# The last step of a seven-product attention block: product A12·B21 moved to the end and finished token tile by token tile, residual buffers moved, GpSimd additions dropped

## The chip, the cores and the metric

One core of one Trainium2 chip runs the whole program. The metric is device time in microseconds (us) of one execution. The kernel before takes 910.19 us, the median of 3 runs (908.84 to 910.43).

## The reference

One layer of neighbourhood attention over 512 tokens (8 rows of 64) with 16 heads of 128, model width 2048, all in float32:

```python
h = rms_norm(x, norm_pre[i])
q, k, v, z = jnp.split(h @ w_in, 4, axis=-1)      # w_in: 2048 x 8192
o = neighbourhood_attention(q, k, v, rpb)
y = (o * jax.nn.silu(z)) @ w_out                  # w_out: 2048 x 2048
x = x + rms_norm(y, norm_post[i])
```

What this case is about is the end: the right half of `y = g @ w_out`, the sum of squares of each row of y, and `x + y * rstd * gain`.

## The kernel before

**Products.** Every float32 operand is split into hi (rounded for TensorE) and lo (the rest), and a product is hi·hi + lo·hi + hi·lo, three matmuls of 128x512 for each tile of 128 tokens. ScalarE makes hi (L231), VectorE makes lo (L232). Ten steps run one behind the other, 512 *slots* in all. Steps 0 and 8 are plain products. Step 9, `LAST`, makes columns 1024 to 2047 of y as a 2x2 block product in seven passes of eight slots (KH = 8, six matmuls per slot); a pass multiplies one combination of blocks of A (the gated attention output) by one combination of blocks of B (w_out). The passes go in this order: A11, S1, A12, N2, A22, N4, N3. Passes 0 and 2 add into chain X in PSUM, 1, 3 and 5 into Y, 4 and 6 into Z (`chain`, L248). `combine` (L317) takes what a chain holds after each pass.

**Operands.** `T[k]` holds a running combination of weight blocks: VectorE adds a freshly loaded block `raw` to it in passes 1, 3 and 4 (L223) and in pass 5 (L239). The `raw` tiles are a ring of four (NRAW), so the load of one waits until the one four earlier has been used up; hi and lo are rings of three. `prep(m)` makes the operands of slot m and is written two slots ahead (AHEAD). The combinations of A stay in SBUF in tiles `a{k}_0` (A11, N4, S1), `a{k}_1` (A12, A22) and `a{k}_2` (N2, N3).

**The end.** Columns of y are four quarters n = 0 to 3 of 512, tokens four tiles t of 128. Step 8 leaves quarters 0 and 1. In step 9, pass A12 completes quarter 2 of tiles 0 and 1, pass N4 quarter 3 of the same tiles, and pass N3 quarters 2 and 3 of tiles 2 and 3. `finish(n, t)` (L646) squares and sums a quarter on ScalarE and multiplies it by the gain on VectorE; with the fourth quarter GpSimd makes the factor `rcy`. `final(t)` (L660) adds the residual: three quarters by one VectorE instruction (L668), the quarter q = 1 by ScalarE (L665) and a GpSimd addition (L666); then the output DMA (L670). In the last pass, the eight slots of tile 2 come first and then the eight of tile 3 (L286 to L292); its operands `w{m}` lie in `a{k}_0`.

**Queues.** All weight and residual loads and most outputs are issued by SyncE (SP), one behind the other. The residual x is loaded by `load_res` (L672), two 256 KB tiles at a time into `a{k}_1`, from slot 33 of step 9 on. A residual tile's 128 partitions read 2 KB each from rows of x that lie 64 rows (512 KB) apart; a raw or T tile is 256 KB in one piece. Engines run in the order in which their instructions stand; a scheduler orders those that the code doesn't pin.

Of the kernel before, what the change touches and what calls it, by code (L numbers as in the profile page):

```python
# [38 lines left out]

NSTEP = HEADS // 2  # L40
# [8 lines left out]
B11, B12, B21, B22 = range(4)  # L49
NRAW = 4  # L50
# [15 lines left out]
def na_block(ctx: ExitStack, tc: tile.TileContext, xT, x, gpre, gpost, w, rpb, mask, out):  # L66
# [43 lines left out]
    for k in range(KH):  # L110
        for n, ops in enumerate(((A11, N4, S1), (A12, A22), (N2, N3))):
            t = ag.tile([P, len(ops), 2, 256], F32R, tag=f"a{k}_{n}", name=f"a{k}_{n}")
            for i, o in enumerate(ops):
                AT[k, o] = (t, i)
# [25 lines left out]
    def split_a(k, src, o, scalar=None, vector=None):  # L140
# [3 lines left out]
        hi, lo = t[:, i : i + 2, 0, :], t[:, i : i + 2, 1, :]  # L144
        (scalar or nc.scalar).copy(hi, src)  # L145
        (vector or nc.vector).tensor_tensor(lo, src, hi.bitcast(F32), ALU.subtract)  # L146

    def take_x(k):
        nc.scalar.activation(X[k], X[k], AF.Copy, scale=gcol[:, k : k + 1])
        split_a(k % KH, X[k], A11 if k < KH else A12)  # L150
# [35 lines left out]
    def where(m):  # L186
# [5 lines left out]
        return step, *divmod(m, KT if step in PLAIN else KH)  # L192
# [7 lines left out]
    for i, m in enumerate(seq):  # L200
        e = max(m - 6, seq[i - NRAW] if i >= NRAW else 0)
# [14 lines left out]
    def prep(m):  # L216
# [63 lines left out]
    def mm_seven(m):  # L280
        step, p, k = where(m)
        c = chain(p)
        if p in (0, 1, 4) and k == 0:
            b = (step + (c == "Y")) % 2
            U[c] = [pm.tile([P, L], F32, tag=f"u{2 * b + s}", name=f"u{step}{c}{s}") for s in range(2)]
        if step == LAST and p == 6:  # L286
            products(m, (0,))
            if k == KH - 1:
                combine_last(0)
                for mm in range(m - KH + 1, m + 1):  # L290
                    products(mm, (1,))
                combine_last(1)  # L292
# [24 lines left out]
    def combine(step, p):  # L317
# [10 lines left out]
        elif p == 2:  # L328
            c["11"] = pair(f"c11_{step}")
            for s in range(2):  # L330
                if step == LAST:
                    finish(2, s, u[s], c["11"][:, s, :])
                else:
                    nc.scalar.activation(c["11"][:, s, :], u[s], AF.Copy, scale=rc[:, s : s + 1])
# [24 lines left out]

    def combine_last(s):  # L360
        u, c = U["Z"][s], C[LAST]
        nc.vector.tensor_tensor(c["21"][:, s, :], u, c["21"][:, s, :], ALU.subtract)
        nc.vector.tensor_tensor(c["22"][:, s, :], c["22"][:, s, :], u, ALU.subtract)
        finish(2, 2 + s, c["21"][:, s, :])
        finish(3, 2 + s, c["22"][:, s, :])
        final(2 + s)
# [386 lines left out]
```

## Time and profile before

| | |
|---|---|
| time, median of 3 runs | 910.19 us (908.84 to 910.43) |
| the profiled execution: its own time | 909.24 us |
| the profiled execution: span from first to last instruction | 907.5 us |
| PE busy share of the span | 97% |
| DVE (VectorE) busy share | 83% |
| ACT (ScalarE) busy share | 62% |
| POOL (GpSimd) busy share | 4% |

The rows are those of the profiled execution; its time is 1.7 us longer than its span and 0.95 us below the median. Times in rows are us from the start of the span. PE is TensorE's matmuls, PEld its weight loads, SPq and ACTq are the DMA issues of SyncE and ScalarE. A row with "x14" merges 14 like instructions, and its duration then runs from the first start to the last end, with the gaps.

### The profile page before, as it was taken

Reading aid. Unit: us, or ns where it says so; the run is one execution under the profiler, and the core shown is the slowest. Engines: PE = TensorE matmul, PEld = TensorE weight load, DVE = VectorE, ACT = ScalarE, POOL = GpSimd, SP = SyncE. Lnnn points to the kernel's source line nnn. Section 1 sums busy time; section 2 is a strip of 40 time slices with the busy share of each in tenths; the row PEclk is TensorE's granted clock in tenths of the full one; section 3 lists DMA queues with packets and bytes.
Section 4 is the critical chain, followed back from the end, with each engine's and each line's share of the span. In section 5 each row is a group of like instructions: output and inputs, shape, how many; then the busy total and the mean of one; then the engine's idle time right before and its main releaser. Section 6 shows DMA issues by size and latency. Waiting matters only on the chain.

```text
span 907.5 us, 13123 instructions
## 1 busy us (share of the span) xinstructions
PE 879.1 (97%) x4184; PEld 729.6 (80%) x4184; DVE 756.4 (83%) x1395; ACT 563.0 (62%) x1077; POOL 36.2 (4%) x63
## 2 busy tenths in 40 slices
PE   9999999999999999999999999999999999999981
PEld 7888888888888888888888888888878888888660
DVE  4477979897988998799879987989799756886877
ACT  6666857585658566755776576758576654455342
POOL 1000000000000000000000000000002000000003
PEclk9999999999999999999999999999999999999996
DMA  8894367637664765476546745773676334544795
GB/s 258 247 266 129 94 183 220 194 101 217 211 173 114 232 203 165 123 233 199 148 148 214 223 140 159 219 209 116 185 255 192 106 117 127 153 137 147 237 219 185
DMA packets 85877, 163.32 MB, mean 180 GB/s; under 512 B 10016, under 2 KB 10016, under 8 KB 85808
## 3 DMA queue, kind: packets, MB, share of 16 engines
q1 hardware_dynamic: 82080, 151.56, 55.8%
q0 software_dynamic: 3296, 10.41, 4.4%
q8 instruction: 32, 0.52, 0.2%
q10 hardware_dynamic: 432, 0.53, 0.2%
q14 instruction: 37, 0.30, 0.1%
HBM read 154.59 MB, written 7.86 MB: 179 GB/s over the span
## 4 chain that ended last, share of the span: by engine, by line
PE 85%; issue 5%; DMA 4%; DVE 3%; POOL 1%; ACT 1%; SPq 0%; DVEq 0%; POOLq 0%; ACTq 0%
PE u L269 19%; PE u1Y L308 4%; PE u4Y L308 4%; PE u5Y L308 4%; PE u6Y L308 4%; PE u3Y L308 4%; PE u2Y L308 4%; DMA raw<-in_w 3%; PE u1X L308 2%; PE u4X L308 2%; PE u3X L308 2%; PE u2X L308 2%; PE u7X L308 2%; PE u5X L308 2%; PE u6X L308 2%
## 5 line engine op out<-in xcount | busy, mean ns | idle before, releaser
L231 ACT CAST hi<-t 128x512 fp32r<-128x512 f32 x312 | 192.0, 618 | 134.4 <-DVE lo L232 26.0
L232 DVE TENSOR_TENSOR lo<-t,hi 128x512 fp32r<-128x512 f32 x312 | 212.8, 688 | 29.8 <-ACT hi L231 29.0
L232 DVE TENSOR_TENSOR lo<-raw,hi 128x512 fp32r<-128x512 f32 x192 | 131.7, 690 | 66.0 <-ACT hi L231 53.2
L231 ACT CAST hi<-raw 128x512 fp32r<-128x512 f32 x192 | 118.7, 620 | 103.9 <-DVE lo L232 23.5
L223 DVE TENSOR_TENSOR t<-t,raw 128x512 f32<-128x512 f32 x192 | 128.4, 688 | 6.3 <-DMA raw<-in_w 5.7
L269 PE MATMUL u<-hi,a 128*128 128x512 f32 x512 | 131.1, 392 | 1.4 <-ACT a L145 0.8
L269 PEld LDWEIGHTS u<-hi,a 128*128 128x128 f32 x512 | 95.0, 188 | 21.5 <-ACT a L145 1.3
L269 PE MATMUL u<-lo,a 128*128 128x512 f32 x256 | 70.8, 390 | 0.0
L269 PEld LDWEIGHTS u<-lo,a 128*128 128x128 f32 x256 | 48.1, 188 | 10.1
L239 DVE TENSOR_TENSOR t<-t,raw 128x512 f32<-128x512 f32 x64 | 42.9, 689 | 7.7 <-DMA raw<-in_w 7.7
L308 PE MATMUL u9Y<-hi,a 128*128 128x512 f32 x96 | 27.0, 398 | 3.6 <-ACT hi L231 3.6
L440 DVE TENSOR_TENSOR bm<-braw,mask_sb 128x256 f32<-128x256 f32 x48 | 27.5, 603 | 0.0
L308 PE MATMUL u1Y<-hi,a 128*128 128x512 f32 x96 | 26.8, 396 | 0.0
L308 PE MATMUL u4Y<-hi,a 128*128 128x512 f32 x96 | 26.8, 396 | 0.0
L308 PE MATMUL u5Y<-hi,a 128*128 128x512 f32 x96 | 26.8, 396 | 0.0
L308 PE MATMUL u3Y<-hi,a 128*128 128x512 f32 x96 | 26.8, 396 | 0.0
L308 PE MATMUL u6Y<-hi,a 128*128 128x512 f32 x96 | 26.8, 396 | 0.0
L308 PE MATMUL u2Y<-hi,a 128*128 128x512 f32 x96 | 26.8, 396 | 0.0
L308 PE MATMUL u7Y<-hi,a 128*128 128x512 f32 x96 | 26.8, 396 | 0.0
L146 DVE TENSOR_TENSOR a<-x,a 128x512 fp32r<-128x512 f32 x16 | 11.0, 690 | 18.2 <-ACT a L145 18.2
L434 POOL DMA_DIRECT2D braw<-in_rpb x16 | 8.6, 535 | 436.1 <-DVE bm L440 252.0
L308 PEld LDWEIGHTS u9Y<-hi,a 128*128 128x128 f32 x96 | 17.6, 188 | 9.2 <-ACT hi L231 5.9
(444 smaller groups left out, 1958.0 us busy)
## 6 DMA issues: line engine op xcount, KB each, us to landing
raw<-in_w SPq DMA_DIRECT2D x384, 256.0 KB, 2.9
t<-in_w SPq DMA_DIRECT2D x128, 256.0 KB, 2.9
x<-in_xT SPq DMA_DIRECT2D x16, 256.0 KB, 5.5
xres<-in_x SPq DMA_DIRECT2D x16, 256.0 KB, 8.2
graw<-zm POOLq DMA_DIRECT2D x14, 256.0 KB, 3.6
out<-xres SPq DMA_DIRECT2D x14, 256.0 KB, 3.0
sq<-in_x SPq DMA_DIRECT2D x6, 512.0 KB, 9.2
braw<-in_rpb POOLq DMA_DIRECT2D x16, 184.0 KB, 3.9
```

What stands on the lines that cost most here:

```text
L146: (vector or nc.vector).tensor_tensor(lo, src, hi.bitcast(F32), ALU.subtract)
L223: nc.vector.tensor_tensor(T[k], T[k], src, ALU.add)
L231: nc.scalar.copy(hi, src)
L232: nc.vector.tensor_tensor(lo, src, hi.bitcast(F32), ALU.subtract)
L239: nc.vector.tensor_tensor(T[k], T[k], src, ALU.add)
L269: nc.tensor.matmul(U[n][j], l, r, start=k == 0 and i == 0, stop=k == KT - 1 and i == 2)
L308: nc.tensor.matmul(U[c][s], l, r, start=p in (0, 1, 4) and k == 0 and n == 0, stop=k == KH - 1 and n == 2, skip_group_check=True,)
L434: nc.gpsimd.dma_start(raw[:, 0 : 7 * TBL + 32], src)
L440: nc.vector.tensor_tensor(bm[:, i, :].rearrange("p (a b) -> p a b", b=8), rev, mask_sb[:, i, :].unsqueeze(2).to_broadcast([P, 32, 8]), ALU ...
```

## The change

- In step 9 the passes go A11, S1, N2, A22, N4, N3, A12 (`LATE`). Quarters 2 and 3 of tiles 2 and 3 are complete after N3, one pass before the end, and quarter 2 of tiles 0 and 1 comes last.
- The last pass takes all eight slots of tile 0, finishes tile 0 (`finish`, `final`), then tile 1. Its operands hi and lo go to the storage of N2 and A22 (`m >= N - KH`), and their `prep` is written beside that of N3, one pass ahead. Chain Z moves to two other PSUM tiles, because X stays open to the end.
- `a{k}_0` is cut in two: A11 alone, and N4 with S1. The split of A's first half into hi and lo (`take`) so becomes two instructions of 256 columns per engine in place of one of 512.
- The residual is loaded one tile per call: tiles 2 and 3 from slot 8 of step 9 on into the A11 storage, tile 1 from slot 16 on into buffers `z`, tile 0 from slot 41 on.
- In `final` all four quarters are VectorE's; ScalarE's scaling and GpSimd's addition go. `finish` no longer waits for the squares before the gain multiplication of quarter 2 from PSUM.

```diff
+LATE = (0, 1, 3, 4, 5, 6, 2)
...
-        for n, ops in enumerate(((A11, N4, S1), (A12, A22), (N2, N3))):
+        for n, ops in enumerate(((A11,), (N4, S1), (A12, A22), (N2, N3))):
...
+    def take(k):
+        if k < KH:
+            split_a(k, X[k][:, 0:256], A11)
+            split_a(k, X[k][:, 256:512], N4)
+        else:
+            split_a(k - KH, X[k], A12)
...
-        e = max(m - 6, seq[i - NRAW] if i >= NRAW else 0)
+        e = max(m - 6 if m < N - KH else 0, seq[i - NRAW] if i >= NRAW else 0)
...
-        if step == LAST and p == 6:
-            t = ag.tile([P, 2, L], F32R, tag=f"a{k}_0", name=f"w{m}")
-            hi, lo = t[:, 0, :], t[:, 1, :]
+        if m >= N - KH:
+            hi, lo = (A(k, o).rearrange("p a b -> p (a b)") for o in (N2, A22))
...
+            if step == LAST and c == "Z":
+                U[c] = [px.tile([P, L], F32, tag="T", name=f"u{step}{c}{s}") for s in range(2)]
+            else:
+                U[c] = [pm.tile([P, L], F32, tag=f"u{2 * b + s}", name=f"u{step}{c}{s}") for s in range(2)]
+        if m >= N - KH:
+
+            s, kk = divmod(2 * k, KH)
+            for j in (kk, kk + 1):
+                products(N - KH + j, (s,))
+            if kk + 2 == KH:
+                finish(2, s, U["X"][s], C[LAST]["11"][:, s, :])
+                final(s)
...
+        elif step == LAST:
+            c["11"] = pair(f"c11_{step}")
+            for s in range(2):
+                dve.tensor_tensor(c["21"][:, s, :], u[s], c["21"][:, s, :], ALU.subtract)
+                dve.tensor_tensor(c["22"][:, s, :], c["22"][:, s, :], u[s], ALU.subtract)
+                finish(2, 2 + s, c["21"][:, s, :])
+                finish(3, 2 + s, c["22"][:, s, :])
...
-            if q == 1:
-                nc.scalar.activation(yg[q, t], yg[q, t], AF.Copy, scale=rcy[:, col])
-                nc.gpsimd.tensor_tensor(r, yg[q, t], r, ALU.add)
-            else:
-                nc.vector.scalar_tensor_tensor(r, yg[q, t], rcy[:, col], r, ALU.mult, ALU.add)
-            eng = nc.scalar if t == 3 and q % 2 else nc.sync
+            dve.scalar_tensor_tensor(r, yg[q, t], rcy[:, col], r, ALU.mult, ALU.add)
+            eng = nc.scalar if t == 1 and q % 2 else nc.sync
...
     for k in range(KH):
-        at(base(LAST) + 4 * KH + 1 + 3 * k // 2, load_res, k)
-    for t in range(2):
-        at(base(LAST) + 6 * KH + t, final, t)
+        t, q = divmod(k, 4)
+        at(base(LAST) + KH + k, load_res, 2 + t, q)
+        at(base(LAST) + (5 * KH + 2 * q + 1 if t == 0 else 2 * KH + 2 * q), load_res, t, q)
+    for s in range(2):
+        at(base(LAST) + 6 * KH + 1 + s, final, 2 + s)
...
     for m in range(-AHEAD, N):
-        if m + AHEAD < N:
+        if m + AHEAD < N - KH:
             prep(m + AHEAD)
+        if N - 2 * KH <= m + AHEAD < N - KH:
+            prep(m + AHEAD + KH)
```

SP's queue near the start of step 9 before; `raw470` is the weight tile of slot 470, and step 9 begins with slot 456:

```order
L212 DMA raw470_8567<-in_w 128x512
L212 DMA raw471_8582<-in_w 128x512
L212 DMA raw472_8595<-in_w 128x512
L212 DMA raw473_8608<-in_w 128x512
L212 DMA raw474_8621<-in_w 128x512
```

The same place now; `xres20` is the residual of tile 2, quarter 0:

```order
L223 DMA raw470_8607<-in_w 128x512
L64 DMA xres20_8617<-in_x 128x1x512
L223 DMA raw471_8624<-in_w 128x512
L64 DMA xres21_8632<-in_x 128x1x512
L223 DMA raw472_8639<-in_w 128x512
L64 DMA xres22_8647<-in_x 128x1x512
L223 DMA raw473_8654<-in_w 128x512
L64 DMA xres23_8662<-in_x 128x1x512
```

Twelve residual tiles have moved up: eight stand one behind each raw from raw470 to raw477, and four more between raw478 and raw485. The last four stand behind raw511, the last weight tile.

VectorE in the same stretch before (`lo466` is the lo operand of slot 466, made from T):

```order
L232 TENSOR_TENSOR lo465_8548<-t1_136,hi465_8547 128x512
L232 TENSOR_TENSOR lo466_8564<-t2_137,hi466_8563 128x512
L232 TENSOR_TENSOR lo467_8579<-t3_138,hi467_8578 128x512
L232 TENSOR_TENSOR lo468_8592<-t4_139,hi468_8591 128x512
L232 TENSOR_TENSOR lo469_8605<-t5_140,hi469_8604 128x512
```

and now:

```order
L242 TENSOR_TENSOR lo465_8588<-t1_144,hi465_8587 128x512
L234 TENSOR_TENSOR t0_143<-t0_143,raw472_8639 128x512
L242 TENSOR_TENSOR lo466_8604<-t2_145,hi466_8603 128x512
L234 TENSOR_TENSOR t1_144<-t1_144,raw473_8654 128x512
L242 TENSOR_TENSOR lo467_8621<-t3_146,hi467_8620 128x512
L234 TENSOR_TENSOR t2_145<-t2_145,raw474_8669 128x512
L242 TENSOR_TENSOR lo468_8636<-t4_147,hi468_8635 128x512
```

Between two lo operands of pass S1 there now stands the addition of a raw tile for pass N2, six slots ahead of the slot whose lo follows it.

VectorE at the end now, from the first residual additions (`u9X0` is chain X of tile 0, `u9X1` that of tile 1):

```order
L64 SCALAR_TENSOR_TENSOR xres32_8707<-s5_9_8722,rcy_154,xres32_8707 128x512
L64 SCALAR_TENSOR_TENSOR xres33_8725<-e_9_8841,rcy_154,xres33_8725 128x512
L64 TENSOR_TENSOR c11_9_9170<-u9X0_8509,gpost2_8072 128x512
L64 TENSOR_SCALAR msy_153<-part_109,ms3_152 128x1
L64 SCALAR_TENSOR_TENSOR xres00_9105<-y0_0_8118,rcy_154,xres00_9105 128x512
L64 SCALAR_TENSOR_TENSOR xres00_9105<-y1_0_8480,rcy_154,xres00_9105 128x512
L64 SCALAR_TENSOR_TENSOR xres02_9156<-c11_9_9170,rcy_154,xres02_9156 128x512
L64 SCALAR_TENSOR_TENSOR xres02_9156<-s1_9_8599,rcy_154,xres02_9156 128x512
L64 TENSOR_TENSOR c11_9_9170<-u9X1_8510,gpost2_8072 128x512
```

The finishing of tiles 2 and 3 (combinations, gains, eight residual additions) stands whole ahead of that of tile 0, and tile 0 ahead of tile 1.

## Rows read from the trace of the kernel before

**Rows 1.** The page: the span, and TensorE's busy time, share and instructions.

```profile
span 907.5 us, 13123 instructions
PE 879.1 (97%) x4184; PEld 729.6 (80%) x4184; DVE 756.4 (83%) x1395; ACT 563.0 (62%) x1077; POOL 36.2 (4%) x63
```

**Rows 2.** Busy time by stretches: the stretch, PE busy (instructions), PEld, DVE, ACT and POOL the same way, PEclk, the DMA share and GB/s.

```profile
820.00:830.00 10.00, 10.00 (x46) 8.29 (x45) 4.88 (x8) 5.76 (x10) 0.00 (x0) 1.00 0.41 114
...
850.00:860.00 10.00, 8.47 (x37) 6.11 (x35) 6.99 (x13) 3.67 (x6) 0.00 (x0) 1.00 0.89 256
860.00:870.00 10.00, 8.41 (x31) 5.53 (x32) 7.34 (x13) 3.59 (x6) 0.00 (x0) 1.00 1.06 272
870.00:880.00 10.00, 8.73 (x35) 5.89 (x33) 6.54 (x11) 3.77 (x7) 0.00 (x0) 1.00 1.06 248
```

**Rows 3.** The timeline of PE, step 9: its first matmuls and its last. Columns: start, duration, engine, line, operation, names, count.

```profile
802.62 1.07 PE L308 MATMUL u9X<-hi,a 128*128 128x512 f32 x4
...
881.94 5.86 PE L308 MATMUL u9Z<-w,a 128*128 128x512 f32 x25
```

**Rows 4.** The timeline of all engines from 885 us to the end, cut to the rows that the sum uses.

```profile
885.57 2.97 POOL L666 TENSOR_TENSOR xres<-y,xres 128x512 f32<-128x512 f32 x2
885.61 1.80 DVE L668 SCALAR_TENSOR_TENSOR xres<-c,rcy,xres 128x512 f32<-128x512 f32 x1
...
889.67 0.74 DVE L668 SCALAR_TENSOR_TENSOR xres<-c,rcy,xres 128x512 f32<-128x512 f32 x1
890.33 0.74 DVE L668 SCALAR_TENSOR_TENSOR xres<-s,rcy,xres 128x512 f32<-128x512 f32 x1
891.00 0.68 DVE L362 TENSOR_TENSOR s<-u9Z,s 128x512 f32<-128x512 f32 x1
891.60 0.67 DVE L363 TENSOR_TENSOR e<-e,u9Z 128x512 f32<-128x512 f32 x1
...
894.12 0.20 DVE L656 TENSOR_SCALAR msy<-part,ms 128x1 f32<-128x1 f32 x1
...
894.39 0.55 POOL L657 TENSOR_TENSOR rcy<-msy,mhalf 128x1 f32<-128x1 f32 x1 [5.86 <-DVE msy L656]
...
894.98 0.75 DVE L668 SCALAR_TENSOR_TENSOR xres<-y,rcy,xres 128x512 f32<-128x512 f32 x1
...
901.51 1.75 DVE L668 SCALAR_TENSOR_TENSOR xres<-e,rcy,xres 128x512 f32<-128x512 f32 x1
```

**Rows 5.** The chain of waits in order of time (start, duration, what): two of its pieces in step 9.

```profile
856.21 6.31 DMA raw<-in_w
...
871.09 8.60 DMA raw<-in_w
```

**Rows 6.** The DMA view of 856 to 872 us, its rate in 40 slices of 0.4 us.

```profile
GB/s 343 394 405 384 220 210 266 246 256 246 256 261 287 399 389 379 389 256 200 220 236 271 236 225 271 271 338 297 205 215 225 251 236 266 230 292 297 328 200 241
```

**Rows 7.** The DMA view of 871.8 to 883 us: rate in 40 slices of 0.28 us, and what was moved.

```profile
GB/s 219 219 219 271 241 256 278 234 263 219 212 278 212 205 241 271 234 285 256 249 256 219 234 241 227 212 256 241 263 263 263 249 263 183 146 132 88 37 0 0
DMA packets 1337, 2.42 MB, mean 216 GB/s; under 512 B 156, under 2 KB 156, under 8 KB 1337
```

**Rows 8.** The DMA view of 803 to 840 us: rate in 40 slices of 0.925 us, and its loads with the median time to landing.

```profile
GB/s 164 0 0 0 0 75 208 177 352 208 295 153 233 0 0 0 0 18 9 0 0 0 51 250 190 133 226 193 140 257 206 166 259 281 337 175 261 210 146 213
...
raw<-in_w SPq DMA_DIRECT2D x19, 256.0 KB, 3.0
```

**Rows 9.** The timeline of DVE and of SP's issues from 806 us: additions to T for pass S1 (L223), lo operands (L232), raw loads.

```profile
806.46 0.69 DVE L223 TENSOR_TENSOR t<-t,raw 128x512 f32<-128x512 f32 x1
...
807.18 25.01 SPq L212 DMA_DIRECT2D raw<-in_w  x14
...
811.32 0.69 DVE L232 TENSOR_TENSOR lo<-t,hi 128x512 fp32r<-128x512 f32 x1
...
811.92 0.69 DVE L223 TENSOR_TENSOR t<-t,raw 128x512 f32<-128x512 f32 x1
...
812.53 0.69 DVE L232 TENSOR_TENSOR lo<-t,hi 128x512 fp32r<-128x512 f32 x1
...
848.97 1.22 DVE L339 TENSOR_TENSOR s<-e,s 128x1024 f32<-128x1024 f32 x1
```

**Rows 10.** Groups of instructions (line, engine, operation, shapes, count, then busy us, mean ns, idle before): a subtraction of 512 columns (the page) and one of 256 (groups by shape).

```profile
L146 DVE TENSOR_TENSOR a<-x,a 128x512 fp32r<-128x512 f32 x16 | 11.0, 690 | 18.2 <-ACT a L145 18.2
```

```profile
L62 DVE TENSOR_TENSOR x<-x,x 128x256 f32<-128x256 f32 x24 | 10.2, 423 | 0.5
```

**Rows 11.** Busy time by stretches, columns as in rows 2, around the other place where A is split.

```profile
690.00:700.00 10.00, 10.00 (x51) 8.50 (x51) 9.97 (x17) 6.88 (x13) 4.36 (x8) 1.00 0.70 190
700.00:710.00 10.00, 9.48 (x42) 7.51 (x41) 9.53 (x17) 8.65 (x16) 1.09 (x2) 1.00 0.58 168
```

More of the change, by code (lines that the diff above doesn't have):

```diff
@@ L143, in split_a @@
         src = src.rearrange("p (a b) -> p a b", b=256)
-        hi, lo = t[:, i : i + 2, 0, :], t[:, i : i + 2, 1, :]
+        n = src.shape[1]
+        hi, lo = t[:, i : i + n, 0, :], t[:, i : i + n, 1, :]
         (scalar or nc.scalar).copy(hi, src)
         (vector or nc.vector).tensor_tensor(lo, src, hi.bitcast(F32), ALU.subtract)
+    def take(k):
[4 more added lines that the diff above has]
+            split_a(k - KH, X[k], A12)
     def take_x(k):
         nc.scalar.activation(X[k], X[k], AF.Copy, scale=gcol[:, k : k + 1])
-        split_a(k % KH, X[k], A11 if k < KH else A12)
+        take(k)
     def sum_x(k):
@@ L191, in where @@
             step += 1
-        return step, *divmod(m, KT if step in PLAIN else KH)
+        p, k = divmod(m, KT if step in PLAIN else KH)
+        return step, LATE[p] if step == LAST else p, k
     def is_raw(m):
@@ L284, in mm_seven @@
             b = (step + (c == "Y")) % 2
[L285 to L292, printed above, removed]
+            if step == LAST and c == "Z":
[9 more added lines that the diff above has]
+                final(s)
         else:
@@ L330, in combine @@
             for s in range(2):
-                if step == LAST:
-                    finish(2, s, u[s], c["11"][:, s, :])
-                else:
-                    nc.scalar.activation(c["11"][:, s, :], u[s], AF.Copy, scale=rc[:, s : s + 1])
+                nc.scalar.activation(c["11"][:, s, :], u[s], AF.Copy, scale=rc[:, s : s + 1])
         elif p == 3:
@@ L358, in combine @@
                 scale_c(c["22"], s, 2)
[L360 to L366, printed above, removed]
     def scale_c(t, s, j):
@@ L549, in fetch_g @@
         nc.gpsimd.dma_start(X[h], graw[h])
-    def take_g(h):
-        split_a(h % KH, X[h], A11 if h < KH else A12)
     beside = {}
@@ L608, in na_block @@
             at(early(h - 5), fetch_g, h)
-            at(early(h - 2), take_g, h)
+            at(early(h - 2), take, h)
         else:
-            at(when(h, 23), take_g, h)
+            at(when(h, 23), take, h)
     pending = {}
@@ L649, in finish @@
         y = yg[n, t] = src if dst is None else dst
-        rest = px.tile([P, L], F32, tag="S", name=f"ysq{n}_{t}") if dst is None else dst
-        nc.scalar.activation(rest, src, AF.Square, accum_out=part[:, t, n : n + 1])
-        if n == 2:
+        rest = px.tile([P, L], F32, tag="S", name=f"ysq{n}_{t}") if n > 1 else dst
+        i = n if n < 2 or t > 1 else 5 - n
+        nc.scalar.activation(rest, src, AF.Square, accum_out=part[:, t, i : i + 1])
+        (dve if n > 1 else nc.vector).tensor_tensor(y, src, gb[n], ALU.mult)
+        if i == 2:
             nc.vector.reduce_sum(ms3[:, col], part[:, t, 0:3], axis=mybir.AxisListType.X)
             nc.vector.tensor_scalar(ms3[:, col], ms3[:, col], 1.0 / D, EPS, ALU.mult, ALU.add)
-        if n == 3:
-            nc.vector.tensor_scalar(msy[:, col], part[:, t, 3:4], 1.0 / D, ms3[:, col], ALU.mult, ALU.add)
+        if i == 3:
+            dve.tensor_scalar(msy[:, col], part[:, t, 3:4], 1.0 / D, ms3[:, col], ALU.mult, ALU.add)
             nc.gpsimd.tensor_tensor(rcy[:, col], msy[:, col], mhalf[:, 0:1], ALU.pow)
-        nc.vector.tensor_tensor(y, src, gb[n], ALU.mult)
     def final(t):
```

18 lines of the change are left out of this document (11 added, 7 removed).

## The prediction

> **What bounds the kernel now.** I read the page first, then busy time by stretches, then the timeline of the last step, the chain of waits and the DMA views. TensorE is busy 97% of the span [rows 1], so only two places can give anything: where it stands still, and what comes behind its last matmul. Both are in step 9. At full pace 46 matmuls pass in the 10 us from 820 [rows 2], 0.2174 us each; a slot of six takes 1.304 us and the 56 slots of step 9 take 73.0 us. The step starts at 802.6 and PE ends at 881.94 + 5.86 = 887.8 [rows 3], so it takes 85.2: 12.2 us are lost, nearly all after 850, where the stretches hold 31 to 37 matmuls instead of 46 [rows 2]. The chain of waits names the cause: weight tiles that take 6.3 and 8.6 us to land [rows 5], against 3.0 when nothing stands ahead of them [rows 8]. The 16 residual tiles share the queue with T and raw there. Behind the last matmul lie 907.5 - 887.8 = 19.7 us, in which VectorE, ScalarE and GpSimd finish four token tiles; beside GpSimd's additions one VectorE residual addition took 1.80 us, alone 0.74 [rows 4].
>
> **The end: what the change removes and adds.** Count from E, the moment at which pass N3 is done and the last pass (48 matmuls, 10.4 us) starts. VectorE's order sets the rest. Two blocks (combine, gain, sums) for tiles 2 and 3: before, one ran from 891.00 to 894.12 with one foreign instruction of 0.6 among it [rows 4], so between 2.5 and 3.1 us; I take 2.95 since the two now stand strictly one behind the other and wait for their squares: 5.9. Eight residual additions at the pace of those that ran alone, 890.33 to 891.00, 0.67 [rows 4]: 5.3, together 11.2. Tile 0: the gain multiplication 0.6, from `msy` over GpSimd's `rcy` to the first addition 894.98 - 894.12 = 0.86 [rows 4], four additions 2.66: 4.1, at 15.3. Tile 1 the same: 19.5. PE has ended at 10.4, so tile 1's sums are there long before. From the end of the last addition to the end of the span it was 907.5 - 903.26 = 4.2 [rows 4]. So the span ends at **E + 23.7**, 13.3 us behind PE instead of 19.7. The removed GpSimd and ScalarE work costs VectorE four more additions (2.7 us); the slow ones beside GpSimd (four at some 1.0 us extra) go. Bounds: 2.5 to 3.3 per block and 0.6 to 0.7 per addition give 22.3 to 25.2.
>
> **When E comes.** Without any wait PE would reach E 48 slots after 802.6: 865.2. What can hold it up is the new place of the loads. Before, the queue was empty from 815 to 822 [rows 8]; twelve residual tiles now fill that hole and more. Their price: in 871.8 to 883, 2.42 MB = 9.2 tiles moved in about 10.5 us of traffic, mostly residual [rows 7]. Unmixed weight tiles pass at some 390 GB/s (the slices with 379 to 405 GB/s in [rows 6]), 0.68 us a tile. With two weight tiles among the 9.2, a residual tile costs (10.5 - 1.4) / 7.2 = 1.27, say 1.3 us, twice as much.
>
> The Trainium skill, page "DMA: Bandwidth & Descriptors", section "Specifications", wants 512 B per transfer for full rate, and a residual tile moves in 2 KB pieces; by that it would cost what a weight tile costs and the time would be that of the first rival below, which the rates in [rows 7] speak against. The same page, section "Latency and other measured facts", reports 207 GB/s for rows 512 KiB apart, which is how the residual is read; that would be 1.27 us a tile, so here the trace agrees.
>
> Now the queue. raw470 is issued at 807.18, since the addition at 806.46 frees its buffer [rows 9]; traffic begins near 808.4 [rows 8], so the first residual tile starts at 809.1. From it to raw485 stand 12 residual and 15 raw tiles: 12 x 1.3 + 15 x 0.68 = 25.8 us; with about 1 us from last byte to landing, raw485 lands at **835.9**. VectorE adds it to T, and in its order 37 instructions stand between the addition at 806.46 and that one; at the pace of 0.605 (811.32, 811.92, 812.53 in [rows 9]) it would be there at 828.8. So it is kept waiting about 7 us, spread over the additions of raw472 to raw485, and what is queued behind each of them is the lo operand that PE needs next. Before, PE had none of this: the S1 additions ran some ten microseconds ahead, and pass A12, which needs no addition, came next.
>
> From the addition of raw485 to the lo operand of slot 503, the last of N3, stand 51 instructions of 512 columns, one of 1024 (1.22 us [rows 9]) and four tiny ones: 30.9 + 1.2 + 0.4 = 32.5 us. This is tight, because the operands of A12 are made in the same stretch as those of N3. I add 1.5 for waits inside it: raw492 and raw506 can only be issued when the tile four earlier is used up, and at 3.0 us to landing [rows 8] each comes 0.6 to 0.9 late. Bounds 0 and 3. Then 1.0 for that lo and the four matmuls behind it. E = 835.9 + 32.5 + 1.5 + 1.0 = **870.9**, 5.7 us of stalls against 12.2 now. TensorE's granted clock stayed at 1.00, its level of 2.4 GHz, through the stalls of before [rows 2], so I price no slower clock.
>
> **Small edits.** Splitting A's first half into two halves: 2 x 0.423 in place of 0.690 [rows 10], 0.15 us for each of 16 pairs, on ScalarE about the same. The eight at the start hide while the input loads: VectorE sits idle for 18.2 us ahead of that line [rows 10]; without that cover 1.2 us. The other eight fall where VectorE is busy 9.97 and 9.53 of 10 us and PE already loses 0.5 [rows 11]: between 0 and 1.5 in all, I take **0.5**. Chain Z in other PSUM tiles, the A11 storage, and the last four residual tiles behind raw511 (needed 11 us after E) I cost at nothing: PE's last pass and VectorE's finishing of tiles 2 and 3 cover the loads; were that cover gone, the first of them would add about its 3 us of landing.
>
> **Sum.** 870.9 + 23.7 + 0.5 = 895.1 of span, plus the 1.7 outside it: 896.8 against 909.24 of the profiled execution, 12.4 less. That execution lies 0.95 below the median of 910.19; on the median's scale 897.8, say **898**. A measurement here can tell about 0.2% (1.8 us) from no change: faster means under 908.4, slower over 912.0.
>
> **Rivals.** (1) *The loads hide.* If a residual tile costs what a weight tile does, 27 x 0.68 + 809.1 + 1 = 828.5, VectorE is never kept waiting, and 828.8 + 32.5 + 1.5 + 1.0 = 863.8 lies under PE's own 865.2. Then 865.2 + 23.7 + 0.5 + 1.7 + 0.95 = 892. For it: the slices with nearly 400 GB/s [rows 6]; against: the mixed ones [rows 7]. (2) *The delay only moves.* If mixing slows every tile to the 248 GB/s of 870 to 880 [rows 2], 262 KB take 1.06 us; raw485 lands at 809.1 + 27 x 1.06 + 1 = 839, E comes 3 us later, and the eight T tiles right behind meet a queue that isn't empty yet (some 2 us): 903. Most of the old stall is then back. (3) *Slower: the ring of four starves VectorE through three passes.* A raw that takes 8.6 us [rows 5] with four in flight means one per 2.15 us where PE needs one per 1.304. If that held for the 25 raws from raw471 to raw495, 0.85 x 25 = 21.2 us, plus 1.8 because N3 then starts with VectorE full (12.2 us of work for 10.4 of matmuls): 865.2 + 23.0 + 23.7 + 0.5 + 1.7 + 0.95 = 915. It turns into a loss from 22 such raws on. Against it: only twelve residual tiles, and the four last ones stand apart. (4) *Nothing gained*: about 19 such raws, or the end isn't shortened because VectorE has taken over GpSimd's share, would leave the time within 0.2%. That the order isn't as the code says is excluded: it stands above.
>
> **How the numbers follow.** Forecast (895 to 902) 0.55, loads hide (892) 0.22, delay moves (903) 0.14, slower 0.05, no change 0.04. The range reaches to both neighbours, with the bounds of the end: 891 to 905. Faster 0.91, same 0.04, slower 0.05.
>
> **What would show it.** In the profile of the changed kernel: PE's last matmul 13 us ahead of the end, and 16 residual additions of VectorE near 0.74 us, none at 1.8; matmul counts under 46 per 10 us between about 815 and 840 with raw tiles landing late, and again near the end of N3; full counts in the last pass; VectorE without a gap from E on. Wrong would be: full counts from 815 to 840 (then rival 1), stalls reaching to 860 (rivals 2 and 3), or VectorE waiting in the last pass for residual tiles.

## The result, and the profile of the changed kernel

The changed kernel takes **902.89 us** (median of 4 runs, 901.65 to 903.68) against 909.52 (908.46 to 910.43) before: ratio 0.9926, 95% interval 0.9908 to 0.9945, 6.6 us or 0.7% faster. The prediction of 898 us had the sign right and its range, 891 to 905, holds the time, but only half of the expected gain came. A second measurement of the same kernel, beside the experiments, gave 901.76 us and the ratio 0.9926 again (0.9900 to 0.9952).

The execution profiled here took 903.68 us, 901.9 of them span. First the first matmuls of three passes, as one tile's instructions on TensorE (duration min/median/max in ns, first start to last start):

```profile
L322 PE MATMUL u1X<-hi,a x64: 389/390/486, 98.4 to 134.5; 128*128 128x512 f32 x64
L322 PE MATMUL u9X<-hi,a x32: 389/389/390, 807.2 to 817.6; 128*128 128x512 f32 x32
L322 PE MATMUL u9Y<-hi,a x96: 387/389/501, 818.1 to 865.8; 128*128 128x512 f32 x96
L322 PE MATMUL u9X<-a,a x32: 389/389/390, 878.3 to 888.7; 128*128 128x512 f32 x32
```

Three things are to be read here. Step 9 begins at 807.2, not at 802.6 as before [rows 3], and step 1 at 98.4 instead of 94.3, so some 4 us went where the change does almost nothing. The first pass of eight slots takes 818.1 - 807.2 = 10.9 us: a slot is **1.36 us**, not the 1.304 of the prediction. And the last pass starts (E) at 878.3, 71.1 us behind the start of the step, where 48 slots at full pace are 65.3: 5.8 us of stalls.

Busy time by 10 us (sum, PE with its matmuls, granted clock, DMA share, GB/s) shows the stalls, as [rows 2] does before:

```profile
810.00:820.00 10.00, 10.00 (x46) 1.00 0.69 196
820.00:830.00 10.00, 9.37 (x40) 1.00 1.06 265
830.00:840.00 10.00, 7.87 (x31) 1.00 1.00 271
840.00:850.00 10.00, 10.00 (x46) 1.00 0.75 239
870.00:880.00 10.00, 9.25 (x41) 1.00 0.51 131
```

They have moved from the stretch 850 to 882 to where the twelve residual loads now are, and come once more at the end of N3. VectorE's timeline gives the pace (start, duration, instruction, in brackets the idle time before it and who ended it):

```profile
819.05 0.69 DVE L234 TENSOR_TENSOR t<-t,raw 128x512 f32<-128x512 f32 x1 [1.26 <-DMA raw<-in_w]
821.00 0.69 DVE L234 TENSOR_TENSOR t<-t,raw 128x512 f32<-128x512 f32 x1 [0.66 <-DMA raw<-in_w]
822.99 0.69 DVE L234 TENSOR_TENSOR t<-t,raw 128x512 f32<-128x512 f32 x1 [0.69 <-DMA raw<-in_w]
824.96 0.69 DVE L234 TENSOR_TENSOR t<-t,raw 128x512 f32<-128x512 f32 x1 [0.67 <-DMA raw<-in_w]
826.95 0.69 DVE L234 TENSOR_TENSOR t<-t,raw 128x512 f32<-128x512 f32 x1 [0.69 <-DMA raw<-in_w]
...
837.10 0.69 DVE L234 TENSOR_TENSOR t<-t,raw 128x512 f32<-128x512 f32 x1 [0.96 <-DMA raw<-in_w]
```

Each addition waits for its raw tile, and they come 1.98 us apart (7.90 us over four): one raw and one residual tile, 0.68 + 1.3, the prices of the prediction. What the prediction did not foresee is at the start. Stretches of 2 us at 44 to 52 (same columns), and under them the waits there (us in total, times, longest):

```profile
44.00:46.00 2.00, 1.62 (x8) 1.00 0.99 218
46.00:48.00 2.00, 0.25 (x1) 0.95 1.02 277
48.00:50.00 2.00, 2.00 (x5) 0.50 0.41 113
50.00:52.00 2.00, 2.00 (x8) 0.70 1.01 316
```

```profile
PE u L279 <- ACT hi L241: 2.1, 1, 2.1
ACT x L159 <- DMA x<-in_xT: 1.9, 1, 1.9
```

ScalarE waits for the last x tile, the operand that TensorE needs is queued behind that, TensorE stops for 2.1 us, and then its granted clock is 0.50, the 1.2 GHz level, for some 3 us. The end of the kernel, with VectorE's last additions and the output transfers:

```profile
884.00 1.41 DVE L64 SCALAR_TENSOR_TENSOR xres<-y,rcy,xres 128x512 f32<-128x512 f32 x2
884.77 12.74 SPq L675 DMA_DIRECT2D out<-xres  x14
...
894.87 1.42 DVE L64 SCALAR_TENSOR_TENSOR xres<-y,rcy,xres 128x512 f32<-128x512 f32 x2 [0.66 <-POOL rcy L667]
896.21 0.75 DVE L64 SCALAR_TENSOR_TENSOR xres<-c,rcy,xres 128x512 f32<-128x512 f32 x1
896.87 0.75 DVE L64 SCALAR_TENSOR_TENSOR xres<-s,rcy,xres 128x512 f32<-128x512 f32 x1
```

All additions take 0.74 to 0.75 (a row with "x2" merges two), none 1.8 as in [rows 4], and the span ends 23.6 us behind E (predicted 23.7).

So the questions were: does the cut of the A tile cost the 4.6 us at the start; are the stalls the residual loads' placing; what do the order and VectorE's taking over of GpSimd's additions bring; and what bounds the tail.

### The profile page after: what moved, and what is told of

It is laid out like the page before. It is cut to its first block, busy times and chain, and to the rows that moved or that the text cites. A ratio compares the mean times of both kernels' runs of the same rounds, so it can differ in the third digit from the quotient of the medians.

```text
span 901.9 us, 13169 instructions
## 1 busy us (share of the span) xinstructions
PE 880.9 (98%) x4184; PEld 731.3 (81%) x4184; DVE 755.3 (84%) x1415; ACT 561.2 (62%) x1089; POOL 29.7 (3%) x59
## 5 line engine op out<-in xcount | busy, mean ns | idle before, releaser
L241 ACT CAST hi<-t 128x512 fp32r<-128x512 f32 x320 | 196.8, 618 | 137.3 <-DVE lo L242 31.1
L242 DVE TENSOR_TENSOR lo<-t,hi 128x512 fp32r<-128x512 f32 x320 | 218.1, 687 | 25.8 <-ACT hi L241 24.9
L242 DVE TENSOR_TENSOR lo<-raw,hi 128x512 fp32r<-128x512 f32 x184 | 125.8, 689 | 62.8 <-ACT hi L241 50.3
L241 ACT CAST hi<-raw 128x512 fp32r<-128x512 f32 x184 | 113.6, 620 | 98.9 <-PE u L279 18.7
L279 PE MATMUL u<-hi,a 128*128 128x512 f32 x512 | 133.1, 397 | 3.4 <-ACT hi L241 2.1
L149 DVE TENSOR_TENSOR a<-x,a 128x256 fp32r<-128x256 f32 (+1 forms) x24 | 11.6, 512 | 19.5 <-ACT a L148 19.5
```

Of the source, the lines that this page charges most:

```text
L241: nc.scalar.copy(hi, src)
L242: nc.vector.tensor_tensor(lo, src, hi.bitcast(F32), ALU.subtract)
L279: nc.tensor.matmul(U[n][j], l, r, start=k == 0 and i == 0, stop=k == KT - 1 and i == 2)
```

## The experiments

Every kernel was measured beside the kernel before on its chip; each ratio is to that. In this table "time" is the median of a kernel's runs; the other columns are read from its one profiled execution, which can lie some us off the median (e9's took 897.78, e4's 901.79). They are us from the span's start; "step" is E less the first matmul of u9X, 65.3 at full pace; "tail" is the end less E; "out" is the end less the first output issue.

| run | time us | u1X | u9X | E | step | tail | out |
|---|---|---|---|---|---|---|---|
| changed kernel | 902.89 | 98.4 | 807.2 | 878.3 | 71.1 | 23.6 | 17.1 |
| e7 the same again | 901.76 | 98.2 | 805.6 | 877.9 | 72.3 | 23.7 | 17.2 |
| e10 x early | 899.62 | 95.3 | 802.5 | 874.6 | 72.1 | 23.6 | 17.2 |
| e4 GpSimd back | 903.41 | 94.8 | 801.9 | 874.6 | 72.7 | 25.4 | 19.9 |
| e2 S1 apart | 901.74 | 94.7 | 804.7 | 877.9 | 73.2 | 23.6 | 17.1 |
| e11 one load in two slots | 898.70 | 95.9 | 804.8 | 875.0 | 70.2 | 23.8 | 17.3 |
| e3 one load in three slots | 894.60 | 95.7 | 803.1 | 869.4 | 66.3 | 23.6 | 17.1 |
| e8 e3, halves together | 894.89 | 95.5 | 803.1 | 869.6 | 66.5 | 23.8 | 17.3 |
| e9 e3, other finishing order | 894.63 | 98.0 | 804.9 | 872.5 | 67.6 | 23.5 | 17.0 |
| e12 e9 and x early | 893.66 | 95.2 | 803.0 | 870.9 | 67.9 | 22.8 | 16.4 |

**The cut alone** (e1), on the kernel before:

```diff
-        for n, ops in enumerate(((A11, N4, S1), (A12, A22), (N2, N3))):
+        for n, ops in enumerate(((A11,), (N4, S1), (A12, A22), (N2, N3))):
...
+    def take(k):
+        if k < KH:
+            split_a(k, X[k][:, 0:256], A11)
+            split_a(k, X[k][:, 256:512], N4)
+        else:
+            split_a(k - KH, X[k], A12)
...
-        split_a(k % KH, X[k], A11 if k < KH else A12)
+        take(k)
...
-            t = ag.tile([P, 2, L], F32R, tag=f"a{k}_0", name=f"w{m}")
+            t = ag.tile([P, 2, L], F32R, tag=f"a{k}_1", name=f"w{m}")
...
-        buf = ag.tile([P, 2, L], F32, tag=f"a{k}_1", name=f"xres{k}")
+        buf = ag.tile([P, 2, L], F32, tag=f"a{k}_2", name=f"xres{k}")
```

> The kernel before, with only the tile of the A operands cut in two, so that the first half of every A tile is split by two copies and two subtractions of 256 columns (w and the residual tiles take the names of the new tiles that they overlay); order, residual loads and final additions as before. Theory (the cut costs the start-up: ScalarE does one more copy for every x tile, the last x tile is late, and TensorE loses its clock in the gap): the first matmul of u9X moves from 802.6 us to about 807, the gap at 45 to 48 us and the granted clock of 0.5 behind it are there, and the time is 913 to 915 us. Rival (the late x tile of the changed kernel comes from the moved loads' jitter and not from the cut): first matmul of u9X at 802 to 804, no gap over 1 us at 45 to 48 us, time 908 to 911 us.

908.68 us, ratio 0.9992 (0.9972 to 1.0013). u1X starts at 95.2 and u9X at 802.8, where the kernel before has 94.3 and 802.6. The theory falls: between these two executions the cut costs 0.9 us in step 0 and 0.2 by step 9, and e5, which has no cut, starts u1X at 95.8.

**Another cut** (e2), which splits nothing at the start:

```diff
-        for n, ops in enumerate(((A11,), (N4, S1), (A12, A22), (N2, N3))):
+        for n, ops in enumerate(((A11, N4), (S1,), (A12, A22), (N2, N3))):
...
-        at(base(LAST) + KH + k, load_res, 2 + t, q)
+        at(base(LAST) + 2 * KH + k, load_res, 2 + t, q)
...
```

> The changed kernel with the A tile cut at another place: A11 and N4 stay in one tile, so that the start-up has one copy and one subtraction of 512 columns per x tile again, and S1 alone gives its room to the eight early residual loads. Since S1 is read one pass later than A11, these loads and the four of tile 1 stand eight slots later. Theory (the cut cost the start-up 4.6 us): first matmul of u9X at 802 to 804, 897 to 900 us, with 70 to 72 us from there to the last pass (stalls moved a pass later, not gone). Rival (jitter, or the cost sits elsewhere in step 0): first matmul of u9X at 806 to 808, 902 to 904 us.

901.74 us, ratio 0.9922 (0.9894 to 0.9951): no gain over the changed kernel. u1X at 94.7 is no better than with the cut (94.8 in e4); u9X at 804.7 lies between both forecasts. Between u1X and u9X this execution takes 710.0 us, the others of the table 706.9 to 708.9; e2 also splits N4 and S1, in steps 0 and 8, by two instructions each time in place of one, and whether that is the cause was not tried. The loads a pass later move the stalls by a pass and make them no smaller (7.9 us).

**The changed kernel again** (e7), unaltered.

> The changed kernel unaltered, once more beside the others. Theory (the 4.1 us lost in step 0 of the profiled execution, by the x tile that landed late at 46 us and the lower clock behind it, are one execution's and not the change's): first matmul of u1X at 94.5 to 96 and of u9X at 802 to 804 instead of 807.2, 71 to 74 us from there to the last pass, 23.6 behind it, profiled time 898.5 to 902.5; median 901 to 903. Rival (the change brings it): u1X at 98 to 99, u9X at 806 to 808.

The gap is there again, the theory's forecast missed:

```profile
L322 PE MATMUL u1X<-hi,a x64: 389/389/486, 98.2 to 134.3; 128*128 128x512 f32 x64
...
46.00:48.00 2.00, 0.53 (x2) 0.96 1.03 287
48.00:50.00 2.00, 2.00 (x6) 0.50 0.55 194
```

But its six runs fall into 903.17 to 903.51 (the profiled one among them) and 900.10 to 900.36. And e1, e3, e4, e6, e8, e9 and e11, whose instructions up to the last step are those of the changed kernel one for one, have a gap of 2 us in e9's profiled execution only (2.1); e11's has 1.2, e4's 0.8, the rest 0.4 or less. e9's profiled execution took 897.78 us, the other four of e9 893.82 to 894.87. So the gap comes in some executions of one and the same code, three of nine here, and costs some 3 us. Whether the kernel before has it as often is not known: two profiles have its start, its own without a gap and e5's with 0.3 us.

**x earlier** (e10):

```diff
-        if 0 <= m and m + 3 < KT:
-            load_x(m + 3)
+        for k in range(KT):
+            if m == (k - 3 if k < 8 else k - 4 if k < 11 else k - 5):
+                if k >= 3:
+                    load_x(k)
```

> The changed kernel with the x tiles 8 to 15 of step 0 issued one slot earlier (8 to 10) and two slots earlier (11 to 15); nothing of the last step altered. Theory (the gap at 45 to 48 us in both profiled executions of the changed kernel is the last x tile, landing 6 us after its issue among raws and squares, and the lower clock behind the gap): no gap over 0.5 us at 44 to 50 us, granted clock 1.00 there, first matmul of u1X at 94 to 95.5 instead of 98.3, 898.5 to 901 us. Rival (the raws of step 0 are what is late, and x only stands before them): the gap stays or moves, 901 to 904 us.

899.62 us, ratio 0.9904 (0.9877 to 0.9931). A gap of 1.3 us stands at 42 to 44, the clock stays at 1.00, u1X starts at 95.3:

```profile
42.00:44.00 2.00, 0.69 (x3) 1.00 0.91 229
44.00:46.00 2.00, 2.00 (x10) 1.00 0.65 191
...
L322 PE MATMUL u9X<-hi,a x32: 389/389/389, 802.5 to 812.9; 128*128 128x512 f32 x32
L322 PE MATMUL u9X<-a,a x32: 389/389/389, 874.6 to 885.0; 128*128 128x512 f32 x32
```

Time as the theory said; the gap is smaller and earlier, and not gone. Since the gap comes only in some executions, one profile without the clock's fall is no proof; the intervals of e10 and e7 overlap. For the prediction this execution is the cleanest: it starts step 9 where the kernel before does, and reaches E at 874.6.

**Residual loads spread** (e3):

```diff
-        at(base(LAST) + KH + k, load_res, 2 + t, q)
-        at(base(LAST) + (5 * KH + 2 * q + 1 if t == 0 else 2 * KH + 2 * q), load_res, t, q)
+        at(base(LAST) + KH + 3 * k, load_res, 2 + t, q)
+        at(base(LAST) + (5 * KH + 2 * q + 1 if t == 0 else 4 * KH + 3 * q), load_res, t, q)
```

> The changed kernel with the twelve early residual loads of step 9 spread: one in every three slots from slot 8 to slot 41, instead of twelve in slots 8 to 22 (the last four as they were). Theory (1.3 us of transfer per residual tile beside 0.68 per raw is more than a slot of 1.36, so the loads starve the additions of S1 and N2): from the first u9X to the last pass 66 to 68 us instead of 71.1, and 898.5 to 900.5 us. Rival (the raws come late by their own latency and ring, whatever lies beside them): 70 to 72 us there and 902 to 904 us. A third (spreading only moves the crowd to N4 and N3, where the eight raws of A12 are loaded too): the stalls show at 850 to 880, 901 to 904 us.

**894.60 us**, ratio 0.9841 (0.9813 to 0.9869), twice the gain of the changed kernel and 4 us under the theory's forecast. Its step came out as forecast; the rest is the start, where the profiled execution has a gap of 0.4 us only and reaches u9X at 803.1. Stretches of e3, then whom VectorE waited for from 805 to 875, in the changed kernel (the longest) and in e3 (the three longest):

```profile
820.00:830.00 10.00, 10.00 (x45) 1.00 0.86 264
830.00:840.00 10.00, 10.00 (x46) 1.00 0.94 273
860.00:870.00 10.00, 9.65 (x43) 1.00 0.60 183
```

```profile
DVE t L234 <- DMA raw<-in_w: 7.7, 9, 1.6
```

```profile
DVE t L249 <- DMA raw<-in_w: 1.6, 2, 0.9
DVE lo L242 <- ACT hi L241: 1.3, 2, 0.7
DVE t L234 <- DMA raw<-in_w: 1.2, 1, 1.2
```

The step takes 66.3 us, 1.0 of it stalls. DMA is as busy as before from 820 to 840 (264 and 273 GB/s), but the additions now wait 1.2 us for raws instead of 7.7. In the new order the stalls were the crowding of the loads.

**One load in two slots** (e11): as e3, with `KH + 2 * k` and `3 * KH + 2 * q`.

> The changed kernel with the twelve early residual loads one in every two slots (slots 8 to 30), between the changed kernel (about one in 1.2 slots, 71 to 73 us from u9X to the last pass) and the spread one (one in three, 66.3). Theory (transfer time: two raws and a residual tile take 2 x 0.68 + 1.3 = 2.66 us, two slots 2.72): 66 to 68 us there, 894 to 897 us. Rival (any residual load between raws delays some addition, whatever the spacing): 68.5 to 70 us there, 897 to 900 us.

898.70 us, ratio 0.9899 (0.9873 to 0.9924), and 70.2 us of step: the sum of transfer times fails, and the rival's 70 is nearer. VectorE still waits 4.4 us for raws in these additions:

```profile
DVE t L234 <- DMA raw<-in_w: 4.4, 8, 1.3
DVE t L249 <- DMA raw<-in_w: 2.3, 2, 1.4
```

A schedule whose transfers fill 2.66 of 2.72 us has no room left for a raw that must wait for its buffer first. That this is the reason is argued; shown is that the step takes 71 to 73, 70.2 and 66.3 to 67.9 us at one load in about 1.2, two and three slots. The 1.6 us within the last group are between executions: e9's instructions up to E are those of e3 in the same order.

**The old order with early, spread loads** (e6): the kernel before with e1's cut, and

```diff
-        at(base(LAST) + 4 * KH + 1 + 3 * k // 2, load_res, k)
+        t, q = divmod(k, 4)
+        at(base(LAST) + KH + 3 * k, load_res, t, q)
+        at(base(LAST) + (5 * KH + 2 * q + 1 if t else 4 * KH + 3 * q), load_res, 2 + t, q)
```

> The kernel before in its old order and with its old division of the last additions, but with the A tile cut and twelve of the sixteen residual loads brought forward and spread (one in three slots from slot 8 to slot 41 of the last step, four in slots 41 to 47), instead of sixteen in slots 33 to 44. Theory (the stalls of the last step before, 9.0 us, are these loads beside the raws, and not the order): 66 to 68 us from the first matmul of u9X to the last pass's end less the pass itself, that is the whole step 78 to 80 us instead of 85.2, time 901 to 904 us, about the changed kernel's; the changed order is then worth only the tail. Rival (the old order stalls for another reason, as the two raws of N3's last operands): 906 to 909 us.

904.58 us, ratio 0.9956 (0.9938 to 0.9974): between both forecasts, nearer the theory's. The step still takes 84.6 us (801.3 to 885.9) against 85.2 [rows 3]; what is gained lies behind it, where tile 0 and 1 go out from 875.95 instead of 886.88 and 14.4 us follow TensorE's end instead of 19.7. But the step is no clean test of the theory, because it loses its time in two places. The first are raws, as the chain of waits (start, duration, what) shows:

```profile
850.00 4.20 DMA raw<-in_w
...
857.72 5.09 DMA raw<-in_w
```

The second is the last pass, which takes 15.4 us (870.5 to 885.9) where 10.9 are full pace:

```profile
874.67 1.80 DVE L676 SCALAR_TENSOR_TENSOR xres<-c,rcy,xres 128x512 f32<-128x512 f32 x1
...
880.08 1.88 DVE L240 TENSOR_TENSOR w<-t,w 128x512 fp32r<-128x512 f32 x3
880.81 5.07 PE L316 MATMUL u9Z<-w,a 128*128 128x512 f32 x14 [2.44 <-DVE w L240]
```

With the residual there early, VectorE's finishing of tiles 0 and 1 stands ahead of its last three lo operands (`w`); it lasts from 872.56 to 880.08, two of its additions slowed beside GpSimd. TensorE stands still for 2.4 us, and from 881.9 to 885.3 its granted clock is 0.50 (a stretch of it, columns as in [rows 2]):

```profile
882.00:884.00 2.00, 2.00 (x7) 1.52 (x6) 0.69 (x2) 0.00 (x0) 0.00 (x0) 0.50 0.98 350
```

So 4.5 of the 8.4 us lost in the step are lost there, and 3.9 before it, where the raws are. The same sixteen loads in the same slots cost 1.0 us in the new order in e3, and 2.6 at most (e12). In the old one the raws and T tiles of A22 and N4 come a pass later, on top of the last eight residual loads: DMA is busy 0.90, 0.96 and 0.85 from 840 to 870, in e3 0.69, 0.84 and 0.60. That this is where the remaining 1.3 to 2.9 us come from is argued; no run tried it by itself. Against e6, the larger part of what the new order is worth is another thing: it makes the operands of the last pass before the first residual addition (in the changed kernel the last of them ends at 877.0, E is 878.3), so finishing does not hold TensorE up there. Without the 4.5 us e6's step would by estimate have been about 80, the upper end of the theory's 78 to 80; a run of the old order with these operands ahead of the additions was not made.

**VectorE alone, in the kernel before** (e5, the edit below), and **GpSimd back, in the changed kernel** (e4, the same edit turned round):

```diff
-            if q == 1:
-                nc.scalar.activation(yg[q, t], yg[q, t], AF.Copy, scale=rcy[:, col])
-                nc.gpsimd.tensor_tensor(r, yg[q, t], r, ALU.add)
-            else:
-                nc.vector.scalar_tensor_tensor(r, yg[q, t], rcy[:, col], r, ALU.mult, ALU.add)
+            nc.vector.scalar_tensor_tensor(r, yg[q, t], rcy[:, col], r, ALU.mult, ALU.add)
```

> The kernel before, with only the last additions changed: all sixteen by VectorE, none scaled by ScalarE and added by GpSimd. Theory: beside a GpSimd addition a VectorE one takes 1.75 to 1.80 us, alone 0.74 (a start every 0.67); three with one slowed take 3.1 us per token tile, four alone 2.7; over four tiles about 1.5 us less on VectorE, which is the last engine there: 907 to 909 us, if the kernel before takes 908 to 910. Rival (VectorE has one addition more per tile and is the last engine already): 910 to 912 us.

> The changed kernel with the old division of the last additions: of each token tile one quarter is scaled by ScalarE and added by GpSimd, three are done by VectorE. Theory (a GpSimd addition beside a VectorE one slows both, 0.74 to 1.8 us, and after TensorE's end one tile of them is bare): the additions of the last tile take 5.4 us instead of 3.0, time 904.5 to 906 us. Rival (the end is set by TensorE and the output transfers, who adds does not matter): 902 to 903.5 us.

e5: 907.31 us, ratio 0.9982 (0.9964 to 1.0000), 1.6 us less and what the theory said, though the interval reaches to no change. In its profile 18.3 us follow TensorE's end instead of 19.7. e4: 903.41 us, ratio 0.9946 (0.9923 to 0.9970). By the time the rival holds: it is half a microsecond above the changed kernel's first measurement and 1.6 above its second, the intervals overlap, and the theory's 904.5 to 906 are missed. But the tail of the profiled execution is 25.4 instead of 23.6. Two rows of e4:

```profile
888.82 1.74 POOL L675 TENSOR_TENSOR xres<-y,xres 128x512 f32<-128x512 f32 x1 [0.83 <-ACT y L674]
889.35 1.75 DVE L64 SCALAR_TENSOR_TENSOR xres<-s,rcy,xres 128x512 f32<-128x512 f32 x1
```

A VectorE addition that starts beside GpSimd's ends 0.5 us behind it and takes 1.75 us instead of 0.74. The last tile's additions so take 3.1 us instead of 2.7, not the 5.4 of the theory; more is lost ahead of them, where a gain multiplication beside GpSimd takes 1.27 us and the first addition starts 6.9 us behind E instead of 5.7.

**Both token tiles together in the last pass** (e8), on e3:

```diff
-            s, kk = divmod(2 * k, KH)
-            for j in (kk, kk + 1):
-                products(N - KH + j, (s,))
-            if kk + 2 == KH:
-                finish(2, s, U["X"][s], C[LAST]["11"][:, s, :])
-                final(s)
+            products(m, (0, 1))
+            if k == KH - 1:
+                for s in range(2):
+                    finish(2, s, U["X"][s], C[LAST]["11"][:, s, :])
+                    final(s)
```

> The changed kernel with spread residual loads (as in the run that spread them), but the last pass does both token tiles together, as every other pass, and finishes both behind it. Theory (the tail is VectorE's: it is busy from the first matmul of the last pass on with the two other tiles until 880.4, where TensorE has ended too, so the first block's early end is not used): 894 to 895.5 us, as with blocks. Rival (the prediction's: the first tile's finishing hides behind the second block): 897.5 to 899 us.

894.89 us, ratio 0.9860 (0.9830 to 0.9890), as e3 with its 894.60. "Token tile by token tile" brings nothing that these runs show. VectorE of e8:

```profile
879.97 0.75 DVE L64 SCALAR_TENSOR_TENSOR xres<-e,rcy,xres 128x512 f32<-128x512 f32 x1
880.80 0.69 DVE L64 TENSOR_TENSOR c<-u9X,gpost 128x512 f32<-128x512 f32 x1
```

The additions of tiles 2 and 3 keep it until 880.7, and by then TensorE has finished both halves.

**Another finishing order** (e9), on e3: the sums of tile 0 before the additions of tile 3, those of tile 1 before the additions of tile 0.

```diff
                 finish(2, s, U["X"][s], C[LAST]["11"][:, s, :])
-                final(s)
+                for t in ((3,), (0, 1))[s]:
+                    final(t)
...
-    for s in range(2):
-        at(base(LAST) + 6 * KH + 1 + s, final, 2 + s)
...
+    at(base(LAST) + 6 * KH + 1, final, 2)
```

> The changed kernel with the spread residual loads, and the order of VectorE's last work changed: the multiplication by gpost and the last sum of squares of token tile 0 before the additions of tile 3, those of tile 1 before the additions of tile 0. Theory (VectorE is the bound of the tail and waits there twice for GpSimd's power, 0.65 us each, with nothing to do): both waits are covered by additions, so 1.0 to 1.5 us less, 893 to 893.8 us. Rival (the sixteen output transfers, 4 MB from 875.9 on at some 300 GB/s, set the end): 894 to 895 us, as without.

894.63 us, ratio 0.9856 (0.9830 to 0.9883): by the time the rival holds. In e3 the last addition starts at 887.95, 18.6 us behind E, in e9 at 889.76, 17.3 behind E: VectorE is 1.3 us earlier, just as the theory has it. The end of this execution is not:

```profile
879.02 11.40 SPq L676 DMA_DIRECT2D out<-xres  x14
...
889.76 0.75 DVE L64 SCALAR_TENSOR_TENSOR xres<-s,rcy,xres 128x512 f32<-128x512 f32 x1
```

From the first output issue it is 17.0 us to the end, in e3 17.1; the column "out" of the table is 17.0 to 17.3 in eight of the nine executions with VectorE alone. The ninth is e12, which has e9's finishing order too:

```profile
877.35 11.39 SPq L676 DMA_DIRECT2D out<-xres  x14
...
888.09 0.74 DVE L64 SCALAR_TENSOR_TENSOR xres<-s,rcy,xres 128x512 f32<-128x512 f32 x1
```

There "out" is 16.4 and the tail 22.8, so 0.8 of the 1.3 us came through. Behind the end of the last addition follow 4.3 us in the changed kernel and in e3, 5.5 in e9 and 4.9 in e12: with VectorE earlier, the outputs queue. So this order is worth 0.1 and 0.8 us in these two executions, and more cannot be read from them.

**All three** (e12: e9 with e10's loads).

> The changed kernel with the spread residual loads, the changed order of VectorE's last work and the x tiles issued earlier, all three. Theory (three separate losses: stalls 5 to 7 us, two bare waits 1.3 us, up to 1.5 us of small gaps at 34 to 48 us in the executions without the long gap): 891 to 893 us. Rival (only the spreading counts): 893.5 to 895 us.

**893.66 us**, ratio 0.9840 (0.9811 to 0.9870), in the rival's range. Best of all by the median, 0.9 us under e3, but their intervals coincide: of the three edits only the spreading is shown to count. Both beat the changed kernel (0.9926, 0.9908 to 0.9945).

## Why the prediction was right, and where it was off

**The sum closes.** 895.1 us of span were predicted and 901.9 measured: +4.1 at the start (807.2 against 802.6, with 0.5 allowed for), +2.8 from there to E (71.1 against 68.3), -0.1 in the tail.

**E was the term mis-sized, by 2.8 to 4.4 us in the four profiled executions with these loads (the changed kernel, e7, e10, e4).** e10 starts step 9 at 802.5, so it can be laid on the prediction's clock. VectorE's rows there:

```profile
832.95 0.69 DVE L234 TENSOR_TENSOR t<-t,raw 128x512 f32<-128x512 f32 x1 [1.10 <-DMA raw<-in_w]
...
837.90 0.69 DVE L234 TENSOR_TENSOR t<-t,raw 128x512 f32<-128x512 f32 x1
...
872.00 0.69 DVE L242 TENSOR_TENSOR lo<-t,hi 128x512 fp32r<-128x512 f32 x1
```

raw485 is added at 837.90 (the third from last of this line's 24 additions) instead of 835.9: +2.0. From there to the end of the last lo operand, 872.69, are 34.8 us against 34.0: +0.8, waits of 2.3 us in place of the 1.5 allowed. From that to E, 874.6, 1.9 against 1.0: +0.9. Together 3.7, which is 874.6 - 870.9. The price per pair was right where pairs follow each other (1.98), so the queue's sum was probably not wrong in its terms but in taking the queue as always full: DMA is busy 1.03 from 820 to 830 in e10 and 0.85 from 830 to 840, while the additions still wait. That is argued from these shares and not tried. The rest went as told: from raw485 on VectorE has no other waits than those 2.3 us up to 872.69, so a late raw in S1 or N2 comes out at E. By its size of E the delay lies at the second rival's (the delay only moves, E 3 us later), whose 903 is also nearest to the measured time; its mechanism, 1.06 us for every tile and 2.12 for a pair, is not what the pairs show.

**The stalls of before were oversized.** A stretch counts every matmul that reaches into it, so 46 in 10 us is not 10/46 us each; with 1.36 us a slot the step before lost 85.2 - 76.2 = 9.0 us, not 12.2. E did not rest on that, since it was counted along VectorE. But full pace reaches E at 867.9 and not at 865.2, so the predicted E holds 3.0 us of stalls; that the prediction names 5.7 and 5.8 were measured is chance. The first rival did rest on the slot: "loads hide" gives 2.7 us more with the right one, 894.7, and that is where e3 came out by spreading the loads.

**The tail, 23.6 against 23.7, came out term by term along VectorE.** The first addition starts at E + 5.7 (5.9 priced), the gain multiplication of tile 0 at 11.0 (11.2), that of tile 1 at 15.1 (15.3), the last addition ends at 19.3 (19.5), and 4.3 follow (4.2). That VectorE alone is shorter holds (e4, e5). The half-blocks of TensorE hide nothing, by the prediction's own sum, in which VectorE comes to tile 0 at 11.2 and TensorE is done at 10.4, and by e8. What the prediction did not see is a second bound close beneath: taking 1.3 us off VectorE's chain gives 0.1 us at the end in e9 and 0.8 in e12, because 5.5 and 4.9 us then follow the last addition in place of 4.3: the outputs queue. An earlier first issue, which now comes 6.5 us behind E, after VectorE's two blocks, would move both bounds; that is argued, and issuing tile 2's outputs before tile 3's block was not tried.

**The start was missed.** "The eight at the start hide" was not contradicted (e1), and the loss lies elsewhere: an x tile that lands late in some executions. By the executions of the same instructions without the gap (e1, e3, e6 and others) the 4.1 us at the start are no price of the change, and without them this execution would have come within 2.7 us of the prediction. What makes it late in one execution and not in the next stays open.

**GpSimd beside VectorE** was priced right: 1.75 us for a VectorE addition beside GpSimd's 1.74 (e4), 0.74 alone. The Trainium skill, page "SBUF — State Buffer", section "Summary: rules for kernel authors", says that when VectorE has two SBUF inputs while GpSimd reads SBUF, the one issued second waits until the first has ended; the trace agrees: in e4 all four such VectorE instructions end 0.5 us behind GpSimd's.

## What to carry to other kernels

Moving loads into a quiet stretch is worth only what the consumers beside them can wait: place them by the time that a load takes beyond what each slot has to spare, and leave room (one in three slots left stalls of 1.0 to 2.6 us in four executions, one in two 4.9, nearly one in each 5.8 to 7.4). When an engine's work is taken off the end, ask what bound lies next beneath: of 1.3 us saved on VectorE 0.1 and 0.8 reached the end, since outputs then queued. When loads come earlier, ask what their consumers will now stand in front of: in e6 the finishing that they released held the last pass's operands up, at a price of 4.5 us. Before a few microseconds are put down to an edit, look at a second execution: 3 to 4 us at the start came and went with the same instructions.

## What the runs showed of the hardware

TensorE's clock fell to its lower level (0.50, 1.2 GHz) behind a standstill of 2.0 to 2.1 us at about 46 us in three executions (the changed kernel, e7, e9), and behind one of 2.0 us in e5 (at 860) and of 2.4 us in e6 (at 878); it was back at 1.00 after 3.4 us, in e5, where another standstill of 0.7 us followed, after 6.8. Behind 1.3 us (e10), 1.2 (e11) and 1.4 (e1, at 859) it stayed at 1.00. A residual tile and an output tile have the same shape and the same row spacing in memory; it is 512 KB only within sets of eight rows, and the next set begins one row (8 KB) on. Read, such a tile cost 1.3 us of the queues (1.98 a pair, less 0.68 for the raw), while sixteen written ones took 17.1 us with the landing of the last, under 1.07 each. So that the spacing is what makes the residual tile dear, as the prediction takes it, is not shown; the 1.27 us that it works out for rows 512 KB apart agree in size.
